# Attention's probabilities times values: another cut of the key axis, the prefix keys in one pass

## The chip, the cores and the metric

One core of a Trainium2 chip runs the kernel. The metric is the device time of one execution in microseconds; less is better. Its engines are TensorE (PE in the profile; PEld are its weight loads), VectorE (DVE), ScalarE (ACT), GpSimd (POOL) and SyncE (SP, which here issues most of the DMAs).

## The reference

One layer of an encoder step. 512 prompt tokens follow 16 learned prefix ("meta") tokens; 64 sample tokens follow 128 cached ones. Both streams go through one attention with two groups of eight heads: differential attention (two softmaxes, subtracted) and latent attention. Prompt query blocks see the prefix, their own chunk of 64 and all earlier chunks; the sample sees the 128 cached keys and its own 64. What the change touches is the last step of each head:

```
p = p[:, :, 0] - lam * p[:, :, 1]
o_d = jnp.einsum('bhqk,bkhe->bqhe', p.astype(vd.dtype), vd)
...
o_m = jnp.einsum('bhqk,bkhe->bqhe', pm.astype(vm.dtype), vm)
```

Then come an output product, a residual, a gated feed-forward and a final norm.

## The kernel before

Nearly every product is kept near fp32 by splitting both factors in a high and a low part (`split`, line 164: ACT writes the high part, DVE source minus high) and summing three passes: high times high, high times low, low times high.

TensorE's order is the order in which the program issues its instructions. Attention is written as generators, the streams of class `Streams` (line 46): `run` resumes the ready stream of the lowest rank; a stream yields an estimated delay, and takes and gives PSUM banks by estimated times. `projections` (rank 9) issues the input projections, `diff_attend` (rank 1) the differential heads, `heads` (20) the latent queries, keys and values, `latent_attend` of head h (rank h) the latent heads, `mix_out` (30) the output product's first half. What a stream issues between two yields stands together on TensorE; a stream that yields 0 and has the lowest rank goes on at once.

`probabilities_times_values` (line 225) ends each of the 16 heads. Before it, a head has written its probabilities to `pt_b[b]` (query block b: 128 queries in rows, keys in columns, 16 prefix keys first) and `p5` (the sample's 64 queries). Key tiles are 128 columns counted from the first prefix key, so tile t holds 16 keys of an earlier block and the fifth holds the prompt's last 16. Four groups follow. Each takes bank `tp`, transposes four blocks into it, evacuates it as `pk..h` (ACT) and `pk..l` (DVE), and then issues the passes of the group before:

- group 0: key tile 0 for four query blocks, later three passes of 512 columns;
- group 1: key tile 1, the same;
- group 2: key tile 2 for three blocks and tile 4 for the last block, later three passes of 384 columns and three with 16 rows and 128 columns;
- group 3: key tile 3 for two blocks and two transposes of `p5` (64 rows high), 320 columns and 64 columns to evacuate, later three passes of 256 columns.

Behind another `yield pace` come group 3's passes and `done` (ACT copies `po` out); then the sample: three passes with 128 rows over the cached keys and three with 80 rows over its own, 64 columns each. `pace` is 1.0 in the differential heads and in the last latent head, and 0 in the other seven latent heads (line 1195). A `yield pace` of 1.0 in a differential head lets about twelve projection passes go between.

Values come to it as `vh` and `vl`. In differential heads `natural` (line 642) transposes them, writes them to the outputs and keeps them; in latent heads `pair_values` (line 1127) makes them from the latent keys `ch`, `cl`, which `latent_keys` (line 974) splits. `sign` (line 970) holds a column of signs that `rope` uses.

Of the kernel before, what the change touches and what calls it, by code (L numbers as in the profile page):

```python
# [23 lines left out]
OWN = NS + NM  # L24
TQ = SEQ + NS
T = NM + TQ
TH = T // 2
TP = T + PAST
# [103 lines left out]
def encoder_step(  # L132
# [228 lines left out]
    with ExitStack() as ph:  # L361
# [17 lines left out]
        def ztile(name="z"):  # L379
            return az.tile([P, T], F32, name=name, tag="z", bufs=Z_BUFS)  # L380
# [13 lines left out]
        lamv = az.tile([P, 2], F32, name="lamv")  # L394
        ones = cp.tile([P, P], F32, name="ones")
# [7 lines left out]
        with tc.tile_pool(name="xn", bufs=1) as xn, tc.tile_pool(name="xc", bufs=1, side="right") as xc:  # L403
# [208 lines left out]
            Q.dma_start(qmask, c_qmask)  # L612
        for e in (V, S, Q):
            e.ordered = False
# [10 lines left out]
        def keys_room(tag, name):  # L625
            return kv.tile([P, TP], F32R, name=name, tag=tag, bufs=2)

# [8 lines left out]
        pt_b = [ap.tile([P, P * (b + 2)], F32, name=f"p{b}") for b in range(4)]  # L636
        for b in range(4):
            G.memset(pt_b[b][:, NM + P * (b + 1):P * (b + 2)], 0.0)
        p5 = ap.tile([NS, OWN + P], F32, name="p5")
        G.memset(p5[:, 0:NM], 0.0)  # L640

        def natural(src32, dst_p, dst_s, keep):
# [4 lines left out]
            for j in range(4):  # L647
                PE.transpose(pa[:, j * P:(j + 1) * P], src32[:, j * P:(j + 1) * P], ident)
            na = ap.tile([P, 4, P], F32, name="na", tag="na")
            V.tensor_copy(na, pa.rearrange("p (j c) -> p j c", j=4))  # L650
            store(dst_p[0:SEQ, :].rearrange("(j p) c -> p j c", p=P), na)
# [5 lines left out]
            PE.transpose(pb[0:OWN, 0:P], src32[:, SEQ:T], ident)  # L657
            nb = ap.tile([OWN, P], F32, name="nb", tag="nb")
            S.activation(nb, pb[0:OWN, 0:P], AF.Copy)
            store(dst_p[SEQ:SEQ + NM, :], nb[0:NM, :])  # L660
            store(dst_s, nb[NM:OWN, :])
# [11 lines left out]
        def keys(h, z, khs, kl):  # L673
# [4 lines left out]
            yield from natural(z, nk_p[:, c], nk_s[:, c], lambda na, nb: None)  # L678
# [7 lines left out]
        def values(h, z, vh, vl):  # L686
# [1374 lines left out]
```

## Time and profile before

| | us |
|---|---|
| device time, median of 3 runs | 2387.84 |
| lowest and highest run | 2387.77, 2390.52 |
| span of the profiled execution (no other time of it is given) | 2389.4 |
| TensorE busy in it | 2361.4 |
| DVE, ACT, POOL busy | 1794.6, 1161.9, 705.5 |

The routine's first call begins at 111 us and its last ends near 784 us; differential heads up to 500 us, latent heads from 584 us. A row of a timeline gives start and length in us, engine, line, operation, output and inputs, rows and columns; x4 means four that were merged. TensorE's instructions overlap: a length takes in the pipeline, and two starts give the pitch. The line is mostly that of a helper (L108 a matmul, L112 a transpose, L125 any other).

### The profile page before, as it was taken

What the parts mean: (1) busy time and instruction counts of PE and PEld (TensorE: products, weight loads), DVE (VectorE), ACT (ScalarE), POOL (GpSimd) and SP (SyncE); (2) the same over time, 40 slices, a digit from 0 to 9 for tenths busy, and PEclk for the clock granted to TensorE, in tenths of its full rate; (3) what the DMA queues carried; (4) which work ended last, traced back from release to release, by engine and by line L of the source; (5) the groups of instructions that cost most, each with busy time, mean ns of one, the idle gap of its engine ahead of it and who ended that gap; (6) DMA issues with size and microseconds to landing.
All of it is one profiled execution on the core that took longest, in us unless ns stands there. A gap on an engine that the chain in (4) does not pass through costs nothing.

```text
span 2389.4 us, 44637 instructions
## 1 busy us (share of the span) xinstructions
PE 2361.4 (99%) x17558; PEld 2330.0 (98%) x17558; DVE 1794.6 (75%) x2878; ACT 1161.9 (49%) x2262; POOL 705.5 (30%) x553
## 2 busy tenths in 40 slices
PE   9999999999999999999999999999999999999998
PEld 8999999999999999999999999999999999999998
DVE  5665656776555788788888888888888888888984
ACT  5544445455444554445545555545545433333444
POOL 0000000020001345554454454554554322222320
PEclk9999999999999999999999999999999999999999
DMA  9423333353223553334434434434434975645432
GB/s 277 125 85 86 93 87 94 94 157 116 89 94 107 168 176 108 120 112 151 154 118 151 155 116 151 163 110 155 160 113 153 324 260 170 227 161 169 159 102 98
DMA packets 330547, 340.93 MB, mean 143 GB/s; under 512 B 22610, under 2 KB 272376, under 8 KB 330304
## 3 DMA queue, kind: packets, MB, share of 16 engines
q1 hardware_dynamic: 328720, 334.30, 43.1%
q0 software_dynamic: 1104, 3.22, 0.4%
q8 instruction: 138, 2.26, 0.4%
q10 hardware_dynamic: 512, 0.55, 0.1%
q14 instruction: 73, 0.60, 0.1%
HBM read 267.21 MB, written 74.15 MB: 143 GB/s over the span
## 4 chain that ended last, share of the span: by engine, by line
PE 58%; DVE 1%; DMA 1%; issue 0%; POOL 0%; ACT 0%; DVEq 0%; POOLq 0%; SPq 0%; ACTq 0%
PE m L1454 38%; PE m L1458 19%; PE m L1860 1%; DVE wl L125 1%; DMA raw<-in_ffn_w_down 1%; PE m L1864 0%; DVE ws L125 0%; DMA b<-sumspill 0%; POOL ws L1414 0%; DVE y L125 0%; ACT b L125 0%; DVE b L125 0%; DVE whole L125 0%; DVE c L125 0%; ACT whole L125 0%
## 5 line engine op out<-in xcount | busy, mean ns | idle before, releaser
L1454 PE MATMUL m<-b,wh 128*128 128x288 f32 x7168 | 1052.5, 296 | 4.1 <-DVE y L125 2.7
L1454 PEld LDWEIGHTS m<-b,wh 128*128 128x128 f32 x7168 | 984.0, 189 | 6.7 <-ACT wh L125 4.2
L1458 PE MATMUL m<-b,wl 128*128 128x288 f32 x3584 | 569.8, 295 | 2.0 <-DVE wl L125 1.9
L1414 POOL TENSOR_TENSOR ws<-raw 128x512 f32<-128x512 f32 (+1 forms) x258 | 366.7, 1430 | 542.0 <-DVE wl L125 237.8
L1458 PEld LDWEIGHTS m<-b,wl 128*128 128x128 f32 x3584 | 509.2, 189 | 3.5 <-DVE wl L125 3.4
L125 ACT ACTIVATE wh<-ws 128x512 fp32r<-128x512 f32 (+1 forms) x339 | 282.9, 845 | 393.9 <-PE m L1454 244.4
L125 DVE TENSOR_TENSOR wl<-ws,wh 128x512 fp32r<-128x512 f32 (+1 forms) x339 | 386.8, 1149 | 98.5 <-ACT wh L125 93.0
L125 DVE TENSOR_TENSOR wl<-raw,wh 128x512 fp32r<-128x512 f32 (+1 forms) x393 | 367.8, 959 | 13.5 <-ACT wh L125 11.1
L125 ACT ACTIVATE wh<-raw 128x512 fp32r<-128x512 f32 (+1 forms) x393 | 230.9, 620 | 291.8 <-PE m L1454 241.6
L108 PE MATMUL ps<-xh,wh 128*128 128x296 f32 (+1 forms) x960 | 217.6, 308 | 1.7 <-ACT wh L125 1.7
L108 PE MATMUL ps<-xl,wh 128*128 128x296 f32 (+1 forms) x960 | 208.4, 298 | 0.0
L108 PE MATMUL ps<-xh,wl 128*128 128x296 f32 (+1 forms) x928 | 202.1, 299 | 0.5 <-DVE wl L125 0.5
L125 DVE TENSOR_TENSOR y<-y,m 128x288 f32<-128x288 f32 x280 | 125.4, 449 | 57.7 <-PE m L1458 56.3
L108 PEld LDWEIGHTS ps<-xh,wh 128*128 128x128 f32 x960 | 155.5, 190 | 5.5 <-ACT wh L125 2.1
L125 DVE TENSOR_TENSOR ws<-ws,raw 128x512 f32<-128x512 f32 (+1 forms) x129 | 111.7, 870 | 60.8 <-POOL ws L1414 58.5
L108 PEld LDWEIGHTS ps<-xl,wh 128*128 128x128 f32 x960 | 155.6, 189 | 0.3 <-DVE xl L125 0.2
L108 PEld LDWEIGHTS ps<-xh,wl 128*128 128x128 f32 x928 | 151.1, 189 | 1.0 <-DVE wl L125 1.0
L125 DVE TENSOR_TENSOR wl<-wr,wh 128x1024 fp32r<-128x1024 f32 (+1 forms) x106 | 111.2, 1050 | 29.8 <-ACT wh L125 28.4
L125 ACT ACTIVATE wh<-wr 128x1024 fp32r<-128x1024 f32 (+1 forms) x108 | 97.3, 903 | 59.2 <-PE ps L108 36.2
L1679 POOL TENSOR_TENSOR c<-c,rb 128x576 f32<-128x576 f32 x42 | 67.1, 1599 | 168.7 <-ACT c L125 168.7
L703 POOL MEMSET bias<- 64x64 f32 x8 | 1.2, 144 | 365.1 <-DMA bias<-tsk 311.6
L125 ACT ACTIVATE parts<-c 128x1 fp32r<-128x1 f32 (+1 forms) x266 | 85.7, 322 | 32.3 <-DVE c L125 26.3
(427 smaller groups left out, 3139.2 us busy)
## 6 DMA issues: line engine op xcount, KB each, us to landing
raw<-in_ffn_w_gate SPq DMA_DIRECT2D x44, 1024.0 KB, 5.9
raw<-in_ffn_w_up SPq DMA_DIRECT2D x44, 1024.0 KB, 6.5
raw<-in_ffn_w_down SPq DMA_DIRECT2D x39, 1024.0 KB, 5.5
partspill<-parts SPq DMA_DIRECT2D x133, 288.0 KB, 2.1
b<-partspill SPq DMA_DIRECT2D x133, 288.0 KB, 6.2
wr<-in_w_in SPq DMA_DIRECT2D x54, 512.0 KB, 3.8
wr<-in_w_out SPq DMA_DIRECT2D x16, 512.0 KB, 4.0
wr<-in_w_out SPq DMA_DIRECT2D x24, 256.0 KB, 3.0
```

Source lines behind the costliest of these rows:

```text
L108: self.tc.keep_in_program_order(self.pe.matmul(out, lhsT, rhs, start=start, stop=stop))
L125: ins = issue(*args, **kwargs)
L703: G.memset(bias[0:64, 464:528], -BIG)
L1414: engine.tensor_tensor(w[:, k:k + m, :], pick(xs), pick(ys), op=op)
L1454: PE.matmul(banks[p], wh[k], x, start=first and new and k == 0 and x is hi, stop=False, skip_group_check=not new)
L1458: PE.matmul(banks[p], wl[k], hi, start=False, stop=last and k == n - 1, skip_group_check=not new)
L1679: engine.tensor_tensor(g[:, f, :], g[:, f, :], rb2, op=ALU.mult)
L1860: PE.matmul(bank[:, c0:c0 + 256], a[:, o:o + n], b, start=k + i == 0, stop=k == len(acts) - 1 and i == 2)
```

## The change

- The key tiles begin at the prompt's first key. Tile t meets query blocks t to 3 alone: passes of 512, 384, 256 and 128 columns, three each. Blocks transposed: four in group 0, three in group 1, three in group 2.
- One of `p5`'s two transposes goes to group 1 (cached keys) and one to group 2 (own keys); both are kept to the end in the groups' `pk` tiles.
- The 16 prefix keys stand three more times at the end of each query block's columns (`thrice`, a copy on POOL in each of four blocks of 16 heads). Group 3 transposes the last 112 columns of each block; rows 64 to 111 are the copies. ACT takes the high part of all 48 rows, 512 columns, and DVE makes the last 16 of them low parts. The values' fifth tile has the sample's own 64 rows and below them high, low and high part of the prefix's values (`stacked_values`), so that one pass with 48 rows and 512 columns gives all three products; it comes behind the `yield pace`.
- The sample, in 15 heads: high and low part of the probabilities stand side by side in one `pk` tile, so a pass of 128 columns gives two products. Four passes, two with 128 rows and two with 64; the two halves are added on DVE. The last head keeps six passes of 64 columns, three with 64 rows.
- `vh` and `vl` are passed whole. `natural` takes its first column and its rest as arguments; in differential heads ACT adds three copies to `z`. The latent keys are ordered prefix and prompt, cached, own, and 48 columns with the copies, so `latent_keys` splits and writes them in more pieces; `ch`, `cl` and `z` are wider. `sign` gets three columns and is loaded behind the masks. The memsets of `pt_b` and `p5` fall away, but one.

The constants are STACK = NS + 3 * NM = 112, PROMPT = 528, OWN_K = 656. The core of the diff, with most unchanged lines left out:

```diff
@@ -222,56 +224,57 @@
...
                 yield 0
-    def probabilities_times_values(pt_b, p5, vkeys, vpast, pool, tbanks, pso, pace, done, own_bank=True):
-        def evac(name, src, rows, cols):
-            hi = pool.tile([P, cols], F32R, name=name + "h", tag="pkh", bufs=3)
-            lo = pool.tile([P, cols], F32R, name=name + "l", tag="pkl", bufs=3)
-            split(hi[0:rows], lo[0:rows], src[0:rows, 0:cols])
-            return hi, lo
-        def times_values(n, p, c0):
-            rows = p[0].shape[0]
-            vh, vl = (v[0:rows] for v in vkeys[n])
-            ph, pl = p
-            for m, (a, b) in enumerate(((vh, ph), (vh, pl), (vl, ph))):
-                PE.matmul(po[:, c0:c0 + ph.shape[1]], a, b, start=(n == 0 and m == 0), stop=(n == 3 and m == 2))
-        def cut(pair, rows, c0, c1):
-            return tuple(t[0:rows, c0:c1] for t in pair)
+    def probabilities_times_values(pt_b, p5, own0, past0, vh, vl, pool, tbanks, pso, pace, done, add=None,
+                                   own_bank=True):
+        def pair(g):
+            return pool.tile([P, 2, 512], F32R, name=f"pk{g}", tag="pk", bufs=3)
+        def times_values(t, pk, cols, c0, first=False):
+            n = cols.stop - cols.start
+            for a, i in ((vh, 1), (vh, 0), (vl, 1)):
+                PE.matmul(po[:, c0:c0 + n], a[:, t, :], pk[:, i, cols], start=first and a is vh and i == 1, stop=False)
+        def times_meta(pk):
+            PE.matmul(po, vh[NS:STACK, 4, :], pk[NS:STACK, 1, :], start=False, stop=True)
         yield from st.take("po")
         po = pso.tile([P, 512], F32, name="po", tag="po")
-        last = []
-        for g, blocks in enumerate((((0, 0), (0, 1), (0, 2), (0, 3)), ((1, 0), (1, 1), (1, 2), (1, 3)),
-                                    ((2, 1), (2, 2), (2, 3), (4, 3)), ((3, 2), (3, 3)))):
+        last, kept = [], []
+        for g, blocks in enumerate((((0, 0), (0, 1), (0, 2), (0, 3)), ((1, 1), (1, 2), (1, 3)),
+                                    ((2, 2), (2, 3), (3, 3)), ())):
             if g:
                 yield pace
...
             yield from st.take(bank)
             tp = tbank()
+            pk = pair(g)
             for n, (t, b) in enumerate(blocks):
-                PE.transpose(tp[:, n * P:(n + 1) * P], pt_b[b][:, t * P:(t + 1) * P], ident)
-            w = len(blocks) * P
-            if g == 3:
-                PE.transpose(tp[:, w:w + NS], p5[:, OWN:OWN + P], ident[0:NS, 0:NS])
-                PE.transpose(tp[0:OWN, w + NS:w + 2 * NS], p5[:, 0:OWN], ident[0:NS, 0:NS])
-                w += NS
-            pair = evac(f"pk{g}", tp, P, w)
-            if g == 3:
-                own = [pool.tile([P, NS], F32R, name="p5" + x) for x in "hl"]
-                split(own[0][0:OWN], own[1][0:OWN], tp[0:OWN, w:w + NS])
+                PE.transpose(tp[:, n * P:(n + 1) * P], pt_b[b][:, NM + t * P:NM + (t + 1) * P], ident)
+            if g in (1, 2):
+                c = (past0, own0)[g - 1]
+                PE.transpose(tp[:, 384:384 + NS], p5[:, c:c + P], ident[0:NS, 0:NS])
+                kept.append(pk[:, :, 384:384 + NS])
+            if g < 3:
+                w = 448 if g else 512
+                split(pk[:, 1, 0:w], pk[:, 0, 0:w], tp[:, 0:w])
+            else:
+                for b in range(4):
+                    w = NM + P * (b + 1)
+                    PE.transpose(tp[0:STACK, b * P:(b + 1) * P], pt_b[b][:, w - NS:w + 3 * NM], ident)
+                S.activation(pk[NS:STACK, 1, :], tp[NS:STACK, :], AF.Copy)
+                sub_lo(pk[96:STACK, 1, :], tp[96:STACK, :], pk[96:STACK, 1, :])
             for a in last:
-                times_values(*a)
-            if g < 2:
-                last = [(g, pair, 0)]
-            elif g == 2:
-                last = [(2, cut(pair, P, 0, 384), P), (4, cut(pair, NM, 384, 512), 384)]
+                a()
+            if g < 3:
+                last = [((lambda a: lambda: times_values(*a)))(a) for a in
+                        (((0, pk, slice(0, 512), 0, True),), ((1, pk, slice(0, 384), P),),
+                         ((2, pk, slice(0, 256), 256), (3, pk, slice(256, 384), 384)))[g]]
             else:
-                last = [(3, cut(pair, P, 0, 256), 256)]
+                last = [lambda: times_meta(pk)]
             st.give(bank, 1.9)
         yield pace
         for a in last:
-            times_values(*a)
+            a()
         done(po, 0, SEQ)
         st.give("po", 1.2)
...
@@ -281,14 +284,32 @@
...
-        n = 0
-        for (vh, vl), (ph, pl) in ((vpast, cut(pair, P, 256, 256 + NS)),
-                                   ([v[0:OWN] for v in vkeys[4]], cut(own, OWN, 0, NS))):
-            for a, b in ((vh, ph), (vh, pl), (vl, ph)):
+        (ph, pl), (sh, sl) = [(k[:, 1, :], k[:, 0, :]) for k in kept]
+        if add:
+            both_parts = po5[:, 0:2 * NS].rearrange("p (a b) -> p a b", a=2)
+            PE.matmul(both_parts, vh[:, 5, :], kept[0], start=True, stop=False)
+            PE.matmul(po5[:, NS:2 * NS], vl[:, 5, :], ph, start=False, stop=False)
+            PE.matmul(po5[:, NS:2 * NS], vl[0:NS, 4, :], sh[0:NS], start=False, stop=False)
+            PE.matmul(both_parts, vh[0:NS, 4, :], kept[1][0:NS], start=False, stop=True)
+            done(po5[:, NS:2 * NS], SEQ, TQ)
+            add(po5[:, 0:NS])
+        else:
+            todo = [(v[:, 5, :], p) for v, p in ((vh, ph), (vh, pl), (vl, ph))]
+            todo += [(v[0:NS, 4, :], p[0:NS]) for v, p in ((vh, sh), (vh, sl), (vl, sh))]
+            for n, (a, b) in enumerate(todo):
...
-                n += 1
-        done(po5[:, 0:NS], SEQ, TQ)
+            done(po5[:, 0:NS], SEQ, TQ)
...
+    def thrice(t, c0, n, copy):
+        copy(t[:, n:n + 3 * NM].rearrange("p (r c) -> p r c", r=3),
+             t[:, c0:c0 + NM].unsqueeze(1).to_broadcast([P, 3, NM]))
+    def stacked_values(vh, vl, src):
+        S.activation(vh[0:STACK], src[0:STACK], AF.Copy, scale=sign[0:STACK, 2:3])
+        sub_lo(vl[0:NS], src[0:NS], vh[0:NS])
+        V.scalar_tensor_tensor(vh[NS:96], src[NS:96], sign[NS:96, 1:2], f32(vh[NS:96]), op0=ALU.mult, op1=ALU.subtract)
...
@@ -610,6 +632,7 @@
...
             Q.dma_start(qmask, c_qmask)
+            load(sign, c_rot)
         for e in (V, S, Q):
...
@@ -633,32 +656,30 @@
-        pt_b = [ap.tile([P, P * (b + 2)], F32, name=f"p{b}") for b in range(4)]
-        for b in range(4):
-            G.memset(pt_b[b][:, NM + P * (b + 1):P * (b + 2)], 0.0)
-        p5 = ap.tile([NS, OWN + P], F32, name="p5")
-        G.memset(p5[:, 0:NM], 0.0)
-        def natural(src32, dst_p, dst_s, keep):
+        pt_b = [ap.tile([P, P * (b + 1) + 4 * NM], F32, name=f"p{b}") for b in range(4)]
+        p5 = ap.tile([NS, NS + P], F32, name="p5")
...
@@ -692,9 +715,10 @@
...
-                split(vh[0:OWN, 4, :], vl[0:OWN, 4, :], nb)
-            yield from natural(z, nv_p[:, c], nv_s[:, c], keep)
+                stacked_values(vh[:, 4, :], vl[:, 4, :], nb)
+            yield from natural(z, NM, slice(NM + SEQ, T + 3 * NM), nv_p[:, c],
+                               ((nv_s[:, c], slice(0, NS)), (nv_p[0:NM, c], slice(NS, NS + NM))), keep)
...
@@ -734,18 +758,20 @@
...
-                dst = p5[:, NM:NM + W] if b == 4 else pt_b[b][:, 0:W]
+                dst = p5 if b == 4 else pt_b[b][:, 0:W]
...
+                if b < 4:
+                    thrice(pt_b[b], 0, W, G.tensor_copy)
...
-                pt_b, p5, [(vh[:, t, :], vl[:, t, :]) for t in range(5)],
-                (vh[:, 5, :], vl[:, 5, :]), ap, [("tp", tbank)], pso, 1.0,
-                lambda po, lo_, hi_: S.activation(o32[:, lo_:hi_], po, AF.Copy))
+                pt_b, p5, 0, NS, vh, vl, ap, [("tp", tbank)], pso, 1.0,
+                lambda po, lo_, hi_: S.activation(o32[:, lo_:hi_], po, AF.Copy),
+                lambda src: V.tensor_tensor(o32[:, SEQ:TQ], o32[:, SEQ:TQ], src, op=ALU.add))
...
@@ -854,8 +880,9 @@
...
-                z = ztile()
+                z = az.tile([P, T + 3 * NM], F32, name="z", tag="z", bufs=Z_BUFS)
...
+                thrice(z, 0, T, lambda o, i: S.activation(o, i, AF.Copy))
...
@@ -985,28 +1010,32 @@
             for i in range(2):
-                split(ch[i][:, 0:T], cl[i][:, 0:T], zs[4 + i])
+                split(ch[i][:, 0:PROMPT], cl[i][:, 0:PROMPT], zs[4 + i][:, 0:PROMPT])
+                split(ch[i][:, OWN_K:TP], cl[i][:, OWN_K:TP], zs[4 + i][:, PROMPT:T])
+                split(*[x[i][:, TP:TP + 3 * NM].rearrange("p (r c) -> p r c", r=3) for x in (ch, cl)],
+                      zs[4 + i][:, 0:NM].unsqueeze(1).to_broadcast([P, 3, NM]))
...
@@ -1033,11 +1062,9 @@
-                pb = [aq[0].tile([P, P * (b + 2)], F32, name=f"p{b}{i}") for b in range(4)]
-                for b in range(4):
-                    G.memset(pb[b][:, NM + P * (b + 1):P * (b + 2)], 0.0)
-                p5 = aq[0].tile([NS, OWN + P], F32, name=f"p5{i}")
-                G.memset(p5[:, 0:NM], 0.0)
+                pb = [aq[0].tile([P, P * (b + 1) + 4 * NM], F32, name=f"p{b}{i}") for b in range(4)]
+                p5 = aq[0].tile([NS, 2 * P], F32, name=f"p5{i}")
+                G.memset(p5[:, NS + P:2 * P], 0.0)
...
@@ -1129,13 +1156,16 @@
...
-            for i, (o, n) in enumerate(tok + [(T, PAST)]):
+            for i, (o, n) in enumerate([(NM + P * j, P) for j in range(4)] + [(OWN_K, STACK), (PROMPT, PAST)]):
...
-                split(vh[0:n, i, :], vl[0:n, i, :], pv[0:n, 0:256])
+                if i == 4:
+                    stacked_values(vh[:, 4, :], vl[:, 4, :], pv[:, 0:256])
+                else:
+                    split(vh[:, i, :], vl[:, i, :], pv[:, 0:256])
...
@@ -1175,8 +1205,10 @@
...
-                dst = p5[:, NM:NM + W] if b == 4 else pb[b][:, 0:W]
+                dst = p5[:, 0:W] if b == 4 else pb[b][:, 0:W]
...
+                if b < 4:
+                    thrice(pb[b], 0, W, G.tensor_copy)
...
@@ -1187,12 +1219,14 @@
...
+                add = lambda src: V.tensor_tensor(o32[:, SEQ:TQ], o32[:, SEQ:TQ], src, op=ALU.add)
...
+                add = None
...
-                pb, p5, [(vh[:, t, c], vl[:, t, c]) for t in range(5)],
-                (vh[:, 5, c], vl[:, 5, c]), aq[0], tbanks, pso, 1.0 * (h == H - 1), done, own_bank=h < H - 1)
+                pb, p5, P, 0, vh[:, :, c], vl[:, :, c], aq[0], tbanks, pso, 1.0 * (h == H - 1), done, add,
+                own_bank=h < H - 1)
...
@@ -2007,9 +2041,10 @@
-    rot = np.ones((P, 1), np.float32)
+    rot = np.ones((P, 3), np.float32)
     for base in (0, 64):
-        rot[base + half:base + 64] = -1.0
+        rot[base + half:base + 64, 0] = -1.0
+    rot[NS:NS + NM, 1:3] = 0.0, -1.0
```

## Rows read from the trace of the kernel before

**Rows 1.** Page, part 1: busy us, share of the span, instructions

```profile
PE 2361.4 (99%) x17558; PEld 2330.0 (98%) x17558; DVE 1794.6 (75%) x2878; ACT 1161.9 (49%) x2262; POOL 705.5 (30%) x553
```

**Rows 2.** TensorE's waits, whole span: total us, times, longest us

```profile
PE m L1454 <- DVE y L125: 2.7, 2, 2.3
...
PE ps L108 <- ACT wh L125: 1.7, 1, 1.7
...
PE po L108 <- DVE pk3l L125: 0.8, 2, 0.5
```

**Rows 3.** Timeline, first differential head, group 2's transposes, group 1's passes

```profile
122.49 0.60 PE L112 MATMUL tp<-ident,p 128*128 128x128 f32 x4
...
123.16 0.40 PE L108 MATMUL po<-pk1l,vh 128*128 128x512 f32 x1
...
123.39 0.40 PE L108 MATMUL po<-pk1h,vl 128*128 128x512 f32 x1
```

**Rows 4.** Timeline, same head, from group 3's transposes to the sample's end

```profile
126.01 0.64 PE L112 MATMUL tp<-ident,p 128*128 128x128 f32 x4
...
126.86 0.34 PE L108 MATMUL po<-pk2l,vh 128*128 128x384 f32 x1
...
127.04 0.34 PE L108 MATMUL po<-pk2h,vl 128*128 128x384 f32 x1
...
128.16 0.43 PE L108 MATMUL ps<-xl,wh 128*128 128x296 f32 x2
128.17 0.48 DVE L125 TENSOR_TENSOR pk3l<-tp,pk3h 128x320 fp32r<-128x320 f32 x1
...
129.52 0.28 PE L108 MATMUL po<-pk3h,vh 128*128 128x256 f32 x1
...
129.64 0.28 PE L108 MATMUL po<-pk3l,vh 128*128 128x256 f32 x1
...
131.76 0.28 PE L108 MATMUL po<-p5h,vh 80*128 80x64 f32 x1
...
132.10 0.52 PE L108 MATMUL ps<-xh,wh 128*128 128x296 f32 x2
```

**Rows 5.** Weight loads by form: busy us, mean ns, idle us before

```profile
L108 PEld LDWEIGHTS po<-p5h,vh 80*128 80x128 f32 x16 | 3.1, 192 | 0.0
...
L108 PEld LDWEIGHTS po<-pk2h,vh 16*128 16x128 f32 x16 | 2.9, 181 | 3.9 <-issue 3.9
...
L112 PEld LDWEIGHTS tp<-ident,p 64*128 64x128 f32 x16 | 2.2, 136 | 2.7 <-issue 2.7
```

**Rows 6.** Timeline, a latent head with pace 0, last evacuation

```profile
612.34 0.64 PE L112 MATMUL tp<-ident,p 128*128 128x128 f32 x4
...
613.07 0.44 ACT L125 ACTIVATE pk3h<-tp 128x320 fp32r<-128x320 f32 x1 [0.95 <-PE tp L112]
...
613.54 0.49 DVE L125 TENSOR_TENSOR pk3l<-tp,pk3h 128x320 fp32r<-128x320 f32 x1 [0.82 <-ACT pk3h L125]
...
614.11 0.39 PE L108 MATMUL po<-pk3h,vh 128*128 128x256 f32 x1
...
614.33 0.28 PE L108 MATMUL po<-pk3l,vh 128*128 128x256 f32 x1
```

**Rows 7.** Timeline, a latent head where TensorE stands, same place

```profile
654.70 0.39 PE L108 MATMUL po<-pk3l,vh 128*128 128x256 f32 x1 [0.47 <-DVE pk3l L125]
```

**Rows 8.** Instructions by form, 110 to 790 us, VectorE and ScalarE

```profile
L125 DVE TENSOR_TENSOR pk1l<-tp,pk1h 128x512 fp32r<-128x512 f32 x16 | 11.0, 690 | 19.7 <-ACT pk1h L125 19.7
...
L125 ACT ACTIVATE pk1h<-tp 128x512 fp32r<-128x512 f32 x16 | 9.5, 592 | 18.1 <-PE tp L112 18.1
...
L125 ACT ACTIVATE o<-po 128x64 f32<-128x64 f32 x15 | 3.2, 213 | 7.3 <-PE po L108 7.3
```

**Rows 9.** Instructions by form, 0 to 800 us, POOL

```profile
L1038 POOL MEMSET p<- 128x112 f32 x8 | 1.2, 188 | 2.7 <-DMA mw<-in_mla_w_ukv 2.7
...
L1354 POOL TENSOR_TENSOR b<-b,b 128x288 f32<-128x288 f32 x1 | 0.8, 811 | 0.8 <-ACT b L125 0.8
```

More of the change, by code (lines that the diff above doesn't have):

```diff
@@ L24 @@
 OWN = NS + NM
+STACK = NS + 3 * NM
 TQ = SEQ + NS
@@ L27 @@
 TH = T // 2
+PROMPT, OWN_K = NM + SEQ, NM + SEQ + PAST
 TP = T + PAST
@@ L379, in ztile @@
         def ztile(name="z"):
-            return az.tile([P, T], F32, name=name, tag="z", bufs=Z_BUFS)
+            return az.tile([P, T + 3 * NM], F32, name=name, tag="z", bufs=Z_BUFS)[:, 0:T]
         def x_room(k, w, name, dtype=F32R):
@@ L394, in encoder_step @@
         lamv = az.tile([P, 2], F32, name="lamv")
+        sign = az.tile([P, 3], F32, name="sign")
         ones = cp.tile([P, P], F32, name="ones")
@@ L625, in keys_room @@
         def keys_room(tag, name):
-            return kv.tile([P, TP], F32R, name=name, tag=tag, bufs=2)
+            return kv.tile([P, 6 * P], F32R, name=name, tag=tag, bufs=2)
         def values_room(tag, name, dtype=F32R):
@@ L635, in encoder_step, with natural @@
                 G.memset(f32(qs[i][c][1][both[1 - c], :]), 0.0)
-        pt_b = [ap.tile([P, P * (b + 2)], F32, name=f"p{b}") for b in range(4)]
-        for b in range(4):
-            G.memset(pt_b[b][:, NM + P * (b + 1):P * (b + 2)], 0.0)
-        p5 = ap.tile([NS, OWN + P], F32, name="p5")
-        G.memset(p5[:, 0:NM], 0.0)
-        def natural(src32, dst_p, dst_s, keep):
+        pt_b = [ap.tile([P, P * (b + 1) + 4 * NM], F32, name=f"p{b}") for b in range(4)]
+        p5 = ap.tile([NS, NS + P], F32, name="p5")
+        def natural(src32, c0, rest, dst_p, stores, keep):
             yield from st.take("na")
@@ L647, in natural @@
             for j in range(4):
-                PE.transpose(pa[:, j * P:(j + 1) * P], src32[:, j * P:(j + 1) * P], ident)
+                PE.transpose(pa[:, j * P:(j + 1) * P], src32[:, c0 + j * P:c0 + (j + 1) * P], ident)
             na = ap.tile([P, 4, P], F32, name="na", tag="na")
             V.tensor_copy(na, pa.rearrange("p (j c) -> p j c", j=4))
-            store(dst_p[0:SEQ, :].rearrange("(j p) c -> p j c", p=P), na)
+            store(dst_p[c0:c0 + SEQ, :].rearrange("(j p) c -> p j c", p=P), na)
             st.give("tp", 1.9)
@@ L656, in natural @@
             pb = tbank("pnb")
[L657 to L661, printed above, removed]
+            n = rest.stop - rest.start
+            PE.transpose(pb[0:n, 0:P], src32[:, rest], ident)
+            nb = ap.tile([P, P], F32, name="nb", tag="nb")
+            S.activation(nb[0:n], pb[0:n, 0:P], AF.Copy)
+            for dst, rows in stores:
+                store(dst, nb[rows, :])
             keep(na, nb)
@@ L677, in keys @@
             yield 2.0
-            yield from natural(z, nk_p[:, c], nk_s[:, c], lambda na, nb: None)
+            yield from natural(z, 0, slice(SEQ, T), nk_p[:, c],
+                               ((nk_p[SEQ:SEQ + NM, c], slice(0, NM)), (nk_s[:, c], slice(NM, OWN))),
+                               lambda na, nb: None)
             yield from st.take("tp")
@@ L965, in rope @@
                 b = a ^ 32
-                S.activation(t[b:b + 32, :], z[a:a + 32, :], AF.Copy, scale=sign[a:a + 32, :])
+                S.activation(t[b:b + 32, :], z[a:a + 32, :], AF.Copy, scale=sign[a:a + 32, 0:1])
             V.tensor_tensor(t, t, at_x["sin"][:, c], op=ALU.mult)
             V.tensor_tensor(dst, dst, t, op=ALU.add)
-        sign = az.tile([P, 1], F32, name="sign")
-        load(sign, c_rot)
         rk, ch, cl, rq = [], [], [], []
@@ L979, in latent_keys @@
             ch.extend([keys_room("kh0", "ch0"), keys_room("kh1", "ch1")])
[L980 removed]
+            cl.extend([keys_room("kl", "cl0"), values_room("vh", "cl1").rearrange("p a b -> p (a b)")])
             rk.extend([rkh, rkl])
@@ L987, in latent_keys @@
                 oth = slice(64 - i * 64, 128 - i * 64)
-                load(f32(rkl[i][oth, :]), kmask[oth, :])
+                load(f32(rkl[i][oth, 0:TP]), kmask[oth, :])
             for i in range(2):
-                split(ch[i][:, 0:T], cl[i][:, 0:T], zs[4 + i])
+                split(ch[i][:, 0:PROMPT], cl[i][:, 0:PROMPT], zs[4 + i][:, 0:PROMPT])
+                split(ch[i][:, OWN_K:TP], cl[i][:, OWN_K:TP], zs[4 + i][:, PROMPT:T])
+                split(*[x[i][:, TP:TP + 3 * NM].rearrange("p (r c) -> p r c", r=3) for x in (ch, cl)],
+                      zs[4 + i][:, 0:NM].unsqueeze(1).to_broadcast([P, 3, NM]))
             yield 3.0
@@ L996, in latent_keys @@
             for i in range(2):
-                split(ch[i][:, T:TP], cl[i][:, T:TP], pk[:, i * P:(i + 1) * P])
-            S.activation(rkh[:, T:TP], pk[:, 2 * P:3 * P], AF.Copy)
+                split(ch[i][:, PROMPT:OWN_K], cl[i][:, PROMPT:OWN_K], pk[:, i * P:(i + 1) * P])
+            S.activation(rkh[:, PROMPT:OWN_K], pk[:, 2 * P:3 * P], AF.Copy)
             for i in range(2):
                 own = both[i]
-                sub_lo(rkl[i][own, T:TP], pk[own, 2 * P:3 * P], rkh[own, T:TP])
+                sub_lo(rkl[i][own, PROMPT:OWN_K], pk[own, 2 * P:3 * P], rkh[own, PROMPT:OWN_K])
             st.give("tp", 3.0)
@@ L1006, in latent_keys @@
             rope(kr, zs[6])
-            S.activation(rkh[:, 0:T], kr, AF.Copy)
-            for i in range(2):
-                G.tensor_tensor(rkl[i][both[i], 0:T], kr[both[i], :], f32(rkh[both[i], 0:T]), op=ALU.subtract)
+            for c, at in ((slice(0, PROMPT), slice(0, PROMPT)), (slice(PROMPT, T), slice(OWN_K, TP))):
+                S.activation(rkh[:, at], kr[:, c], AF.Copy)
+                for i in range(2):
+                    G.tensor_tensor(rkl[i][both[i], at], kr[both[i], c], f32(rkh[both[i], at]), op=ALU.subtract)
             yield 6.0
@@ L1153, in queries_keys @@
                 mm3([ps[:, 0, 0:TPH], ps[:, 1, 0:TPH]], wh[:, k], wl[:, k],
-                    halves(ch[k]), halves(cl[k]), k == 0, k == 1)
+                    halves(ch[k][:, 0:TP]), halves(cl[k][:, 0:TP]), k == 0, k == 1)
                 if k == 0:
```

1 line of the change is left out of this document (removed).

## The prediction

> **What bounds the kernel now.** Three views, in this order. The page's first part says that TensorE is busy 99% of the span [rows 1], so the first question is whether anything else is ever late. TensorE's own waits answer it: the longest is 2.7 us, the whole list a few us, and of the routine that is rewritten there is one entry, 0.8 us in two heads [rows 2]. Third comes the timeline of one call of that routine, read for its pitch: with a full TensorE an instruction costs the distance to the next start, not the length in its own column, which takes in the pipeline. So all through attention the end is set by the sum of TensorE's pitches plus the moments at which it stands. Whatever the change adds or takes there moves the end one for one; ACT, DVE and POOL count only where TensorE comes to wait for them.
>
> **Pitches.** A 512-column pass takes 0.23 us (123.16 to 123.39), and four transposes 0.44: from the first of them to the second pass is 0.67, less one pass [rows 3]. A 384-column pass takes 0.18, a 256-column pass 0.12, a projection pass of 296 columns 0.136 (ten of them from 128.16 to 129.52). Passes of 64 columns take 0.11 (three from 131.76 to 132.10), no less than their weight load [rows 4]. A 128-column pass I price at 0.11 as well: it streams half as long as one of 256, so its load decides too.
>
> **Changes of height.** Two stretches cost more than their pitches. From 126.01 to 126.86 stand four transposes, two of them 64 rows high, and one 384 pass: 0.44 + 0.18 = 0.62, but 0.85 passes, 0.23 over. From 126.86 to 128.16 stand two 384 passes, the three 16-row passes and two projection passes: 0.36 + 0.33 + 0.27 = 0.96, but 1.30 passes, 0.34 over [rows 4]. The weight loads say why: the first 16-row load idles 3.9 us in 16 heads (0.25 each) and the first 64-row load 2.7 us, with no engine named; the 80-row loads idle 0.0 [rows 5]. So going to 64 rows or fewer and back makes the weight load wait until the array has run empty; 80 rows do not. The Trainium skill, "TensorEngine Tiling (Array Packing)", Key Properties, says that changing the tiling mode drains TensorE, and under Tiling Modes it lists 64- and 32-row modes; by that the new 48- and 64-row passes pay as the 16-row ones do, which no row here shows.
>
> **TensorE's account of one head.** Before, passes: 6 x 0.23 + 3 x 0.18 + 3 x 0.12 + 3 x 0.11 + 6 x 0.11 = 3.27; height 0.23 + 0.34 = 0.57; together 3.84. After, passes: 3 x (0.23 + 0.18 + 0.12 + 0.11) + 0.23 for the prefix + 4 x 0.11 for the sample = 2.59. Transposes cancel: 16 before and after, 14 full and 2 of p5. So 0.68 a head is saved on passes. But the changes of height go from two to four:
> - p5's two transposes stood together and now stand one in each of two groups. The pair sent 64 columns each, so it was some 0.11 shorter than two full ones and hid that much of its cost; one alone is worth about 0.29, twice 0.58.
> - The prefix pass (48 rows, 512 columns). Bounds: 0, if its height costs nothing, and 0.40. The 16-row run pays about 0.20 on the way in (run empty, then an uncovered load) and 0.14 on the way out, where its short passes were bound by loads anyway; a long pass would pay 0.20 both ways. I take 0.40.
> - The sample's last two passes (64 rows). Bounds 0 and 0.34; I take 0.30, between the two measured.
>
> After: 2.59 + 1.28 = 3.87, +0.03 a head, 15 heads +0.4. The last head keeps six sample passes (+0.22) at 0.34: about +0.3. **Sum of TensorE's own work: +0.7 us.** The saving is eaten.
>
> **The wait that appears.** In the fourth group the prefix keys' transposes go through ACT (512 columns) and DVE (512 columns) before the one prefix pass can start. Seven latent heads call the routine with a pace of 0, and lat[h] has the lowest rank among ready streams, so nothing is put between. The trace shows that order: in the head at 612 the pass on pk3 follows the 16-row run with no projection pass between [rows 6]. There the evacuation was covered by three 384 passes, the 16-row run and both changes of height, and was smaller: ACT 0.44, DVE 0.49. From the first transpose of the group, s = 612.34, ACT started at 0.73 and DVE ended at 1.69, while TensorE wanted pk3l at 1.99 [rows 6]: 0.30 to spare. After: transposes 0.44, six passes 0.69, running empty and loading 0.20: TensorE is ready at s + 1.33. ACT starts at s + 0.69, takes 0.59, DVE 0.69 [rows 8]; with the steps between (0.05 each) the pair is there at s + 2.05. TensorE stands 0.72 us. Five heads: 3.6. In two heads ACT and DVE were still busy with the rotary splits and TensorE stood already; one is in [rows 7], 0.47, the other is its like. Their 0.30 of cover goes too, 1.0 each: 2.0. **+5.6 us**, behind which queue every stream's matmuls, since TensorE's order is the program's.
>
> In the eight differential heads (pace 1.0) twelve projection passes stand before the prefix pass. In the head at 126 DVE's pk3l ended 2.64 after the first transpose, and 0.99 before its pass [rows 4]. After, it ends about 0.3 later, 2.95; TensorE arrives at 0.44 + 0.69 + 12 x 0.136 + 0.20 = 2.96. Just covered there, a little late in heads with a fuller queue: bounds 0 and 8 x 0.3; I take +0.5. The last latent head (pace 1.0) likewise.
>
> **The rest, at or near nothing.** 64 copies on POOL (thrice on p): between 0.19 us (a MEMSET of 128x112) and 0.81 (a sum of 128x288) each, on an engine 30% busy over the span [rows 1, 9], and each is due only in the fourth group, after three groups of other work; without that cover each head would pay it. The copy on z, the wider nb, the third values instruction and the sum of high and low are small (about 0.2 us, as ACT's 128x64 [rows 8]) and hidden behind projection passes, except at the start, where TensorE once waits 1.7 us for ACT's weight split [rows 2]: +0.3. The latent keys are split in more pieces, eight small ones once, behind the output product's passes. The load of sign moves on SP behind the masks and ahead of the next weight loads, one tiny DMA, inside the same +0.3; kernel memsets fall away on POOL, which idles.
>
> **Sum:** 0.7 + 5.6 + 0.5 + 0.3 = +7.1 us. The page gives the profiled span, 2389.4, and no time around it; it lies 0.07% above the median of the runs, 2387.84, so I add the difference to the median: **2394.9 us**. About 0.2% (4.8 us) is what a measurement of this kernel can tell.
>
> **Rivals.**
> 1. *Height is free for the new passes.* For: the rows show only 16-row passes and 64-row transposes. Against: both idle, at every one of 16 heads. Then 0.40 + 0.30 fall away in each head, -11.2, but TensorE is 0.2 earlier at the latent wait, +1.4: 2385.1, not slower. The Trainium skill, "TensorE: Matmul & The Clock Gate", in the table on what matters for kernels, says that one small-K matmul takes the same time as one with K of 128; by that rule this rival is the forecast. The 0.34 above speaks against it.
> 2. *The latent wait is covered.* If something stands between the six passes and the prefix pass (six passes of 0.136 would do), +1.5 is left: 2389.3, no change. Against: the rank rule and the rows.
> 3. *Both:* 2387.8 + 1.5 - 11.2 = 2378, faster.
> 4. *ACT and DVE late in every head,* behind a weight split, as in two heads before: ten more heads by 0.7: about 2402.
>
> **Chances.** Forecast 0.60, first rival 0.15, second 0.12, both 0.05, fourth 0.08. Faster by over 0.2% (below 2383.1): 0.05 and under half of the first, 0.10. Within: the rest of the first, the second, and the forecast's low end (bounds of the three height prices), 0.29. Slower: 0.61. The range takes in the first rival and most of the fourth: 2384 to 2401.
>
> **What would show it.** Right: weight loads of the 48-row prefix pass and the 64-row sample pass that idle about 0.2 with no engine named, and the load behind each as well; single 64-row transposes in two groups; TensorE's waits with a new entry, the prefix pass behind DVE's lower part, some 5 us over 7 heads between 585 and 785 us; the passes' own pitch down by 0.68 a head. Wrong: no idle at those loads (first rival), projection or score passes ahead of the prefix pass in latent heads (second), or a time below 2385.

## The result, and the profile after

The changed kernel was slower: 2398.89 us (median of six runs, 2395.84 to 2403.51) beside 2387.81 for the kernel before on the same chip, a ratio of 1.0040 [1.0029, 1.0051]. Run again on another chip (e7 below), with its profile, it took 2397.16 beside 2390.47, a ratio of 1.0030 [1.0020, 1.0041]. The forecast, 2394.9 on 2387.84, is a ratio of 1.0030. The profiled execution of the first job took 2401.5 us, 2399.7 of it span.

The busy times of the page, beside [rows 1]:

```profile
PE 2363.1 (98%) x17496; PEld 2327.8 (97%) x17496; DVE 1792.1 (75%) x2893; ACT 1163.9 (48%) x2259; POOL 724.3 (30%) x606
```

TensorE's busy time says nothing here: it grew by 1.7 us, with 62 instructions fewer, while the span grew by ten. Its waits say more. Beside [rows 2], where the routine had 0.8 us in two waits, there is now, at the top of the list:

```profile
PE po L110 <- DVE pk L127: 8.0, 10, 1.5
...
PE ps L110 <- ACT wh L127: 1.7, 1, 1.7
```

What such a wait looks like: the head that answers to [rows 6], from the fourth group's transposes on.

```profile
611.46 0.60 PE L114 MATMUL tp<-ident,p 128*112 128x128 f32 x4
...
612.16 0.59 ACT L127 ACTIVATE pk<-tp 48x512 fp32r<-48x512 f32 x1 [1.01 <-PE tp L114]
...
612.43 0.27 PE L110 MATMUL po<-pk,vl 128*128 128x128 f32 x1
612.79 0.70 DVE L127 TENSOR_TENSOR pk<-tp,pk 16x512 fp32r<-16x512 f32 x1 [1.04 <-ACT pk L127]
613.54 0.18 PEld L110 LDWEIGHTS po<-pk,vh 48*128 48x128 f32 x1 [0.97 <-DVE pk L127]
613.54 0.50 PE L110 MATMUL po<-pk,vh 48*128 48x512 f32 x1 [0.83 <-DVE pk L127]
```

ACT begins 0.70 behind the first transpose (forecast 0.69) and the prefix pass 2.08 behind it (forecast: the pair is there at 2.05). Between the six passes and the prefix pass stands nothing, as the rank rule said. In the head like [rows 7], ACT and DVE are late as well, and TensorE stands almost twice as long:

```profile
652.39 0.68 ACT L127 ACTIVATE rq1m<-zr 64x576 fp32r<-64x576 f32 x1
...
653.10 0.59 ACT L127 ACTIVATE pk<-tp 48x512 fp32r<-48x512 f32 x1
653.11 0.75 DVE L127 TENSOR_TENSOR rq1s<-zr,rq1m 64x576 fp32r<-64x576 f32 x1 [0.52 <-ACT rq1m L127]
...
653.89 0.70 DVE L127 TENSOR_TENSOR pk<-tp,pk 16x512 fp32r<-16x512 f32 x1
...
654.65 0.49 PE L110 MATMUL po<-pk,vh 48*128 48x512 f32 x1 [1.49 <-DVE pk L127]
```

The weight loads by form (busy, mean ns, idle before), beside [rows 5]:

```profile
L114 PEld LDWEIGHTS tp<-ident,p 64*128 64x128 f32 x32 | 4.3, 136 | 5.3 <-issue 5.3
L110 PEld LDWEIGHTS po<-pk,vh 64*128 64x128 f32 x17 | 3.2, 195 | 0.0
L110 PEld LDWEIGHTS po<-pk,vl 64*128 64x128 f32 x16 | 3.0, 190 | 0.7
L110 PEld LDWEIGHTS po<-pk,vh 48*128 48x128 f32 x16 | 2.9, 183 | 10.5 <-DVE pk L127 9.7 <-issue 0.7 <-DVE xg L127 0.2
```

p5's 64-row loads idle 5.3 us where they idled 2.7: twice as many, 0.17 each. The 16-row loads, 3.9 us, are gone. The 48-row load stands in the wait, and the sample's 64-row loads hardly idle. What those cost is read from pitches, in a differential head:

```profile
127.06 0.44 PE L110 MATMUL ps<-xh,wl 128*128 128x296 f32 x2
127.60 0.50 PE L110 MATMUL po<-pk,vh 48*128 48x512 f32 x1
128.03 0.54 PE L110 MATMUL ps<-xh,wh 128*128 128x296 f32 x2
128.41 0.44 PE L110 MATMUL ps<-xl,wh 128*128 128x296 f32 x2
...
129.77 0.22 PE L110 MATMUL po<-pk,vh 128*128 128x128 f32 x1
129.83 0.47 PE L110 MATMUL po<-pk,vl 128*128 128x64 f32 x2
130.14 0.30 PE L110 MATMUL po<-pk,vh 64*128 64x128 f32 x1
130.37 0.54 PE L110 MATMUL ps<-xh,wh 128*128 128x296 f32 x2
130.75 0.43 PE L110 MATMUL ps<-xl,wh 128*128 128x296 f32 x2
```

The 48-row pass takes 0.43 to the next start where a 512-column pass takes 0.23, and the two projection passes behind it take 0.38 where two take 0.27. In this head the pass also waits a tenth for its pair, so the two passes ahead of it take 0.54. In five others, where it doesn't wait, the projection pass ahead takes 0.09 more than usual; 0.20, 0.11 and 0.09 are about 0.4 (0.38 by the medians of the pitches). The sample's four passes take 0.60, and the two projection passes behind them again 0.38 where two take 0.27.

One thing no step of the forecast had. The windows view of the latent heads' stretch (length, busy us of each engine, granted clock PEclk as a share of 2.4 GHz, DMA) of this execution reads

```profile
585.00:785.00 200.00, 188.77 (x1303) 177.72 (x1303) 112.34 (x226) 91.48 (x191) 17.11 (x38) 0.97 0.30 95
```

where the kernel before had 1.00. Two windows hold all of the difference:

```profile
655.10:658.50 3.40, 3.40 (x16) 3.34 (x15) 0.00 (x0) 0.60 (x1) 0.00 (x0) 0.50 0.02 5
716.60:723.40 6.80, 6.80 (x29) 6.60 (x29) 2.34 (x4) 1.54 (x3) 0.00 (x0) 0.50 0.20 70
```

They begin 0.5 us behind the wait of 1.49 that ends at 654.65 and 1.7 us behind the second longest, 1.30, that ends at 714.85. In them the clock is at 1.2 GHz. The execution has a gain to set against it: the kernel before (and e7 below) had two such stretches of 3.4 us at 11 and 22 us, and this one had none, which made its first transpose 1.8 us earlier.

### The profile page after: what moved, and what is told of

The parts are those of the page before. It is cut to its first block, busy times and chain, and to the rows that moved or that the text cites. A ratio compares the mean times of both kernels' runs of the same rounds, so it can differ in the third digit from the quotient of the medians.

```text
span 2399.7 us, 44640 instructions
## 1 busy us (share of the span) xinstructions
PE 2363.1 (98%) x17496; PEld 2327.8 (97%) x17496; DVE 1792.1 (75%) x2893; ACT 1163.9 (48%) x2259; POOL 724.3 (30%) x606
## 5 line engine op out<-in xcount | busy, mean ns | idle before, releaser
L127 DVE TENSOR_TENSOR wl<-ws,wh 128x512 fp32r<-128x512 f32 (+1 forms) x339 | 378.7, 1125 | 99.6 <-ACT wh L127 96.6
L305 POOL COPY p<-p 128x48 f32<-128x48 f32 x64 | 21.4, 335 | 552.2 <-DVE p L127 475.4
```

Of the source, the lines that this page charges most:

```text
L127: ins = issue(*args, **kwargs)
L305: copy(t[:, n:n + 3 * NM].rearrange("p (r c) -> p r c", r=3), t[:, c0:c0 + NM].unsqueeze(1).to_broadcast([P, 3, NM]))
```

## The experiments

**My theory:** the loss is the wait for the prefix keys' evacuation, some 6 to 7 us, and what the clock gives away behind it; TensorE's own work comes out even, because four changes of height a head eat what the passes save. **Rivals:** the heights are free and the waits are all of it; the passes save little; the clock falls by chance. Each kernel was timed beside the kernel before in five rounds; e1 to e4, e5 to e7, and e8 and e9 each share a chip. "Stretch" is the time from the first head's first transpose to the last head's last one in the profiled execution (before: 667.3), less 1.6 us where twelve projection passes more lie in it.

| kernel | ratio to before, 95% | us by it | stretch | half clock in the latent heads, us |
|---|---|---|---|---|
| after | 1.0040 [1.0029, 1.0051] | +9.5 | 677.0 | 3.4 and 6.8 |
| e7 after, again | 1.0030 [1.0020, 1.0041] | +7.2 | 673.6 | none |
| e1 after, covered | 1.0003 [0.9995, 1.0012] | +0.7 | 669.6 | 3.4 |
| e2 two heads covered | 1.0011 [1.0002, 1.0020] | +2.6 | 671.3 | none |
| e6 five heads covered | 1.0023 [1.0012, 1.0035] | +5.5 | 672.3 | 6.8 |
| e3 before, 80 rows | 0.9987 [0.9979, 0.9996] | -3.1 | 664.9 | none |
| e8 before, whole | 0.9979 [0.9970, 0.9988] | -5.0 | 662.1 | none |
| e4 after, full rows | 0.9986 [0.9977, 0.9995] | -3.3 | 663.9 | 3.4 and 3.4 |
| e9 e1 and p5 whole | 0.9966 [0.9954, 0.9979] | -8.1 | 659.9 | none |
| e5 e4 and e1 | 0.9935 [0.9920, 0.9951] | -15.5 | 654.6 | none |

**e1 covers the wait.** The yield in front of the prefix pass is held for the latent heads too, so that other streams' passes go between:

```diff
-        yield pace
+        yield max(pace, hold)
         for a in last:
             a()
...
-                own_bank=h < H - 1)
+                own_bank=h < H - 1, hold=1.0)
```

> The changed kernel, with a pace of 1.0 ahead of the prefix pass in the seven latent heads too, so that some twelve passes of other work stand there. If the loss is TensorE's wait for VectorE at that pass (0.85 to 1.56 us in seven heads, 7.4 together) and the half clock behind the two longest waits (about 3): back by 9 to 10 us, near 2389 to 2390, within 0.2% of the kernel before, no half clock between 585 and 785 us. If the loss is TensorE's own work and the waits have only taken the place of others: no more than 2 us back, 2397 or later.

Measured 1.0003: the loss is gone, and the wait has left the head of the list. First in it are now these:

```profile
PE m L1488 <- DVE y L127: 1.9, 2, 1.6
PE m L1492 <- DVE wl L127: 1.8, 5, 0.7
PE ps L110 <- ACT mw L127: 1.8, 2, 0.9
```

Of the 7 to 9 us all but about 1 hangs on that one place. One half-clock stretch is left in the latent heads, at 773.8, where the expectation had none. The order of passes changed and nothing was added, so it was a matter of what stands between and not of ACT's and DVE's work as such.

**e2 and e6 cover two heads, or the other five:** `hold=1.0 * (h in (2, 4))` (the two long waits) and `hold=1.0 * (h not in (2, 4))`.

> The changed kernel, with the cover in two latent heads alone, numbers 2 and 4, those in which ACT and VectorE are busy with the rotary splits and TensorE stands 1.3 to 1.5 us. If the clock falls because of those two waits: 2.9 us of wait and about 3 us of half clock come back, 2393, granted clock 1.00 between 585 and 785 us, and a smaller scatter of the runs than the changed kernel's 2395.8 to 2403.5. If the clock falls for another reason: only the waits come back, 2396, with the scatter as it was.

> The kernel after, with other work ahead of the prefix pass in the five latent heads whose wait is 0.8 us; the two whose wait is 1.3 to 1.5 us are left as they are. If the lowered clock follows the two long waits alone: TensorE's wait for DVE's pk falls from 8 to about 4 us, both half-clock stretches behind the long waits stay, and the time falls by some 4 us against the kernel after, ratio to before 1.0025 to 1.003. Rival, that the clock falls because of all the waits together: the half-clock stretches go too, -7 or more, ratio 1.0015 or lower.

e2's waits are 2.3 us shorter than e7's, which by itself would bring +7.2 to +4.9; it came out at +2.6 [0.5, 4.8], and its profile has no half clock in the latent heads. That leans to the expectation in which the clock is part of the loss, but e7's +7.2 has an interval of its own, [4.8, 9.8], so the times alone don't show it. The wait list reads

```profile
PE po L110 <- DVE pk L127: 5.8, 8, 1.1
```

e6 fits less well. Its waits fell as forecast:

```profile
PE po L110 <- DVE pk L127: 3.6, 4, 1.6
```

and its ratio, 1.0023, stands beside the theory's 1.0025 to 1.0030, though its interval, from 1.0012, takes in the rival's 1.0015. The gain on e7 is only 1.7 where 4 were expected, and the intervals overlap. Its profile has 6.8 us of half clock behind the long wait that ends at 655.08, and none behind the second. By time alone five covered heads are not told from none; the stretch, 1.3 shorter in spite of a fall that e7's execution did not have, leans to the theory.

**e7 is the changed kernel once more.**

> The changed kernel itself, beside the others on this chip: ratio to before 1.003 to 1.005 as before; two half-clock stretches right behind the two longest waits for DVE's pk, if they belong to the program. Rival: the clock's falls come at random, then they stand elsewhere or are missing.

The time repeated; the half clock in the latent heads did not. The waits are the same (one of 1.62 us ends at 657.84), and the window of the latent heads has the clock full:

```profile
PE po L110 <- DVE pk L127: 8.1, 10, 1.6
```

```profile
585.00:785.00 200.00, 188.19 (x1334) 176.86 (x1332) 115.29 (x229) 93.67 (x194) 18.49 (x38) 1.00 0.31 97
```

So neither theory of the clock stands as written: the falls in the latent heads are not in every execution, and yet in three kernels that keep the long waits (after, e4, e6) all five begin 0.5 to 1.7 us behind one of the two, so that five of the eight long waits in these four executions were followed by a fall. (The only one elsewhere, e1's at 773.8, begins 1.2 us behind a wait of 0.8 for mh.) A long wait goes ahead of the fall, but does not always bring it. What decides was not found. The Trainium skill, "TensorE: Matmul & The Clock Gate", Part 1 (The HAM clock gate), says that the gate's look at the engine runs free of the kernel's start; by that the same wait would meet it at another moment in each execution, which fits e7 and which no run here shows.

**e3 takes the 16-row passes' height away** in the kernel before: the fifth key tile's passes take 80 rows of the same operands. The further rows meet nothing but zeros.

```diff
-                last = [(2, cut(pair, P, 0, 384), P), (4, cut(pair, NM, 384, 512), 384)]
+                last = [(2, cut(pair, P, 0, 384), P), (4, cut(pair, OWN, 384, 512), 384)]
```

> The kernel before, with one edit: the three passes over the last 16 keys of the prompt take 80 rows in place of 16 (the probabilities of the other 64 rows are zeros). If a pass of 64 rows or fewer costs a change of height (0.34 us for the run of three) and 80 rows cost none: 16 x 0.34 = 5.4 us faster, 2382.4. If a pass with few rows costs what one with many does: no change, 2387.8.

Measured -3.1 [-5.0, -1.0]. Height costs, so the first rival of the forecast falls. Per head it gives back what [rows 4] had, where nothing turns it into a wait:

```profile
124.98 0.34 PE L108 MATMUL po<-pk2l,vh 128*128 128x384 f32 x1
...
125.95 0.43 PE L108 MATMUL ps<-xl,wh 128*128 128x296 f32 x2
```

Between the same two passes [rows 4] have 1.30, here it is 0.97, and so in all nine heads with a pace of 1.0: 0.33 each, 3.0 us. In the seven other latent heads only 0.00 to 0.19 comes back, 0.8 us in all, because the cover shrinks: TensorE comes earlier to the passes on pk3h and pk3l, and there it stands. Its wait for pk3l grows from 0.8 [rows 2] to

```profile
PE po L108 <- DVE pk3l L125: 1.2, 3, 0.5
```

**e4 takes every change of height out of the changed kernel.** Zeros fill up p5 to 128 rows, the sample's passes and the prefix pass to 112:

```diff
-                PE.transpose(tp[:, 384:384 + NS], p5[:, c:c + P], ident[0:NS, 0:NS])
+                PE.transpose(tp[:, 384:512], p5[:, c:c + P], ident)
...
-            PE.matmul(po, vh[NS:STACK, 4, :], pk[NS:STACK, 1, :], start=False, stop=True)
+            PE.matmul(po, vh[0:STACK, 4, :], pk[0:STACK, 1, :], start=False, stop=True)
...
-            PE.matmul(both_parts, vh[0:NS, 4, :], kept[1][0:NS], start=False, stop=True)
+            PE.matmul(both_parts, vh[0:STACK, 4, :], kept[1][0:STACK], start=False, stop=True)
```

> The changed kernel, with every change of height taken away: p5 has 128 rows (64 of zeros) and is transposed whole, the prefix pass and the sample's last passes take 112 rows, the rest zeros. If the four changes of height cost 2 x 0.29 + 0.38 + 0.26 = 1.22 us a head: 19.5 us less of TensorE's own work, of which the latent wait takes back about 1.4, so 2381, and the latent waits longer than before, with the half clock still there. If they cost nothing: 2399.

Measured 0.9986, faster than before, but well short of what was expected. TensorE got to the prefix pass earlier and waited for it more (with its other waits of over 0.15 us, 17.9 us in the stretch, against 13.4 in the changed kernel's first profile), and in the profiled execution the clock fell behind both long waits, as in the changed kernel:

```profile
PE po L110 <- DVE pk L127: 9.6, 12, 1.7
```

**e5 is e4 with e1's hold**, the two terms taken away together.

> The kernel after with both terms taken away: no pass or transpose of 64 rows or fewer is left in the routine (zeros fill 112 or 128 rows), and other work goes between in front of the prefix pass. My theory: the two are separate terms. Against the kernel after, -19 us of changes of height and -8 to -10 us of waits (DVE's part of the prefix keys) and of lowered clock behind them; the cover leaves some 1 to 2 us of other waits. Against the kernel before on this chip: -12 to -16 us, ratio 0.993 to 0.995, no 'po <- DVE pk' of more than 2 us in all. Rival: the waits only move (the work that goes between is missing later, or banks are given back later), then no better than without the cover: ratio 0.998 to 0.999.

Measured 0.9935 [0.9920, 0.9951], 2376.8 us: the fastest of all, and 12 us better than e4. The wait list keeps little of the routine, the 112-row loads idle a tenth of a microsecond each, and the windows view has the clock full in the latent heads:

```profile
PE po L110 <- ACT o L127: 1.7, 2, 0.8
...
PE po L110 <- DVE pk L127: 1.5, 5, 0.5
```

```profile
L110 PEld LDWEIGHTS po<-pk,vh 112*128 112x128 f32 x33 | 6.1, 189 | 3.3 <-issue 3.3
```

```profile
585.00:785.00 200.00, 192.55 (x1431) 187.46 (x1430) 122.94 (x240) 98.14 (x205) 26.46 (x52) 1.00 0.34 108
```

**e8 does the same for the kernel before:** 80 rows as in e3, and p5 of 128 rows, so that its transposes are whole.

```diff
-                PE.transpose(tp[:, w:w + NS], p5[:, OWN:OWN + P], ident[0:NS, 0:NS])
-                PE.transpose(tp[0:OWN, w + NS:w + 2 * NS], p5[:, 0:OWN], ident[0:NS, 0:NS])
+                PE.transpose(tp[:, w:w + P], p5[:, OWN:OWN + P], ident)
+                PE.transpose(tp[0:OWN, w + P:w + 2 * P], p5[:, 0:OWN], ident)
```

> The kernel before without its own changes of height: 80 rows in place of 16 in the fifth key tile's passes, and p5 padded with zeros to 128 rows, so that its two transposes are whole. It prices the change's saving by itself: e5_full_rows_cover against this one is the same work with 3.27 against 2.59 us of passes a head and no change of height in either. My theory: e5 ran at 0.9935 of the kernel before; the saving of 0.68 a head, 16 heads, is 11 us, and the heights of the kernel before are worth some 4 to 6 us (3 of them seen in e3), less a little for a longer transpose; so this kernel runs at 0.9975 to 0.9985, between e5 and the kernel before, about 9 us above e5. Rival: the cut of the key axis saves little, and e5 won by its heights alone; then this kernel is within 3 us of e5, at 0.995 or lower.

Measured 0.9979, as expected. Between it and e5, where neither has a change of height or a wait of a microsecond in the routine, lie 10.5 us by the ratios, some 4 either way by their intervals (7.5 by the stretches): what the new cut of the key axis saves in passes, forecast at 0.68 a head, 10.9 for 16.

**e9 takes one height out of e1:** p5 has 128 rows and whole transposes; the 48- and 64-row passes stay.

> e1_cover_all with one height term taken away: p5 has 128 rows with zeros, its transposes are whole; the 48-row prefix pass and the 64-row sample passes stay. My theory: two single 64-row transposes a head cost 0.29 each, 16 heads, 9.2 us; from e1's ratio of 1.0003 to 0.996 to 0.997. Rival: TensorE's wait only moves to the evacuations behind the transposes (ACT and DVE have the same work and come no earlier): under 4 us, ratio above 0.9985.

Measured 0.9966, 8.9 us below e1, the expected 9.2. A group with one 64-row transpose in the changed kernel, and the same group in e9:

```profile
607.48 0.69 PE L114 MATMUL tp<-ident,p 128*128 128x128 f32 x4
608.10 0.62 PE L110 MATMUL po<-pk,vh 128*128 128x384 f32 x2
608.56 0.33 PE L110 MATMUL po<-pk,vl 128*128 128x384 f32 x1
```

```profile
602.67 0.60 PE L114 MATMUL tp<-ident,p 128*128 128x128 f32 x4
603.02 0.59 PE L110 MATMUL po<-pk,vh 128*128 128x384 f32 x2
603.46 0.33 PE L110 MATMUL po<-pk,vl 128*128 128x384 f32 x1
```

From the first transpose to the third pass 1.08 and 0.79: 0.29 for one transpose of 64 rows, though it sends half the columns.

## Why the prediction was right, step by step

| step | forecast, us | measured |
|---|---|---|
| p5's single transposes, each | 0.29 | 0.29 in place; 8.9 for 32 by removal (e9), 0.28 |
| prefix pass of 48 rows, over its pitch | 0.40 | 0.38 in place |
| sample's four passes, height included | 0.74 | 0.60, and 0.11 to the passes behind |
| 16-row run of the kernel before | 0.34 | 0.33 in nine heads (e3), 0.11 in the seven where it becomes a wait |
| passes saved a head | 0.68 | 0.66 by the ratios of e5 and e8 (10.5 for 16), 0.50 by their stretches (7.5 for 15) |
| TensorE's own work, sum | +0.7 | about 0 in the differential heads, -1 with the latent heads |
| latent heads' wait | +5.6 | +6.1 |
| differential heads' wait | +0.5 | +0.7 |
| start | +0.3 | +0.4 |
| sum | +7.1 | +6.7 and +11.1 (medians), +7.2 and +9.5 (ratios) |

- **The wait** was the loss, at the place and for the reason given. Seven latent heads stand 0.83 four times, 0.78, 1.49 and 1.30, 6.9 in all, against 0.8 before. The forecast had 0.72 for an ordinary head. The difference is in the load: it counted the prefix pass's weight load into the time before the pair is there, but the rows at 613.54 show load and pass waiting together, though the values had long been ready. Of the wait list's other three entries two are differential heads a little late, 0.34 each, within the bounds of 0 to 2.4. The third, 0.42 at 780.68, is in the first group of the last latent head and isn't new; in the kernel before it stands under another name:

```profile
PE po L108 <- DVE pk0l L125: 0.4, 1, 0.4
```

- **The own work** came out even, as forecast. From the first differential head's first transpose to the first latent head's, e7 takes 0.1 us longer than the kernel before, and no longer once TensorE's waits are taken off both. Over the whole stretch it is 6.3 longer at the same clock, and the waits in it grew by 7.2 (6.9 to some 14.1, counting those over 0.15 us), so about -1 is left, all of it in the latent heads; part of it is the 0.09 of the pass ahead, which a prefix pass that waits does not cost. The three prices of height and the old 16-row run's each came out within 0.04 of the forecast. Two of its signs did not come as written: the 48-row loads idle behind DVE for the most part and not with no engine named, and the sample's 64-row loads idle 0.0 and 0.7 us in all; their price shows in the pitches alone.
- **The rivals.** "Height is free" falls with e3, e8 and e9. "The latent wait is covered" falls with the rows at 613.54; e1 is the kernel in which it holds, and it came out at +0.7 where that rival said +1.5. "Both" is nearest to e5, which had to be built, and which loses p5's heights as well. "Late in every head" did not come: an ordinary latent head waits 0.83 at most, and of the differential heads two wait, 0.34 each.
- **What was missing** is the clock. In the first profiled execution 10.2 us at half clock go with a stretch 3.4 longer than in e7's execution of the same kernel. It is no part of the forecast's sum. The six runs of the first job go with their mean clock, 2395.84 at 0.999 and 2403.51 at 0.995. Whether it is all of the difference between the two ratios, 2.3 us with overlapping intervals, was not shown.

The rule of the Trainium skill, "TensorEngine Tiling (Array Packing)", Key Properties, that a change of tiling mode drains TensorE, agrees with e3, e4, e8 and e9: 16-, 48- and 64-row instructions pay, and 80-row loads idle 0.0. The Trainium skill, "TensorE: Matmul & The Clock Gate", Why this matters for your kernels, has a table by which one matmul with small K takes the time of one with K of 128; in the full stream here it did not: 0.43 to the next start for the 48-row pass, 0.23 for a pass of 128 rows and as many columns.

## What to carry to other kernels

Where TensorE is full, a change that drops passes and brings ones with few rows in their place has to be priced by changes of height as well as by columns: here four of them cost 1.1 to 1.2 us a head, and zeros up to 112 or 128 rows took most of that away for a little POOL time. A pass moved to the end of a chain of transpose, ACT and DVE needs as much other work in front of it as that chain is long; a single yield held back at the right place (e1) was worth some 7 us. Take away one cost of two and the other grows into part of the gap (e4): only both together (e5, -15.5) beat the kernel before by much.

## What was not expected of the hardware

- The granted clock fell to 1.2 GHz behind waits of 1.3 to 1.7 us in some executions and not in others, for 3.4 or 6.8 us at a time. That isn't new with the change: the kernel before has 3.4 us at half clock at 1875.2, 0.3 us behind its wait of 2.3 for y [rows 2], and e3, which stood 2.4 us there, has none. At half clock a projection pass of 288 columns takes 0.24 instead of 0.13 to the next start:

```profile
655.68 0.68 PE L110 MATMUL ps<-cql,mw 128*128 128x288 f32 x2
656.16 1.16 PE L110 MATMUL ps<-cqh,mw 128*128 128x288 f32 x4
```

From the first row to the second two passes take 0.48. By that pitch a stretch of 3.4 us costs 1.5; the three such in the first profile went with 3.4, 1.1 each.
- 112 rows cost next to nothing in a full stream, but a pass that had to wait pays for its weight load as well. In e5 the 112-row pass of 512 columns takes 0.24 to the next start where it comes without a wait, as one of 128 rows does (0.23), and 0.31 where it waited:

```profile
591.25 0.40 PE L110 MATMUL po<-pk,vh 112*128 112x512 f32 x1
591.49 0.42 PE L110 MATMUL ps<-cqh,mw 128*128 128x288 f32 x2
...
607.25 0.47 PE L110 MATMUL po<-pk,vh 112*128 112x512 f32 x1 [0.23 <-DVE pk L127]
607.56 0.49 PE L110 MATMUL ps<-ch,kw 128*128 128x360 f32 x2
```

So it is in all sixteen heads, nine without a wait and seven with one. Heights taken away by padding return less (0.35 a head from e9 to e5 by the stretches) than their price in place (0.38, and 0.26 for the sample, whose four passes with the excess of the pass behind take 0.70 in the changed kernel and 0.44 in e5). More than half of what is missing went into waits: e5 has 12.4 us of them in the stretch, e9 9.7, 0.18 more a head. Where the rest went is not shown.
